# Scan of a hybrid decoder layer: products with the states for both halves first, then one run of 64-column products

## The chip, the cores and the metric

The kernel runs on one core of one Trainium2 chip. The metric is the device time of one execution in microseconds (us). Before the change, three runs took 1005.76, 1002.24 and 1003.0 us; their median is 1003.0 us.

## What is computed

One decoder layer over 512 tokens and 16 learned leading tokens, with 1024 channels: a norm, one wide input projection, two mixing branches side by side (causal pooling, and a Mamba-2 state-space scan), their gated sum, and a squared-ReLU MLP. The change lies in the scan. It has 32 heads of 64 channels in 8 groups of four heads, and works in chunks of 128 tokens:

```python
cb = jnp.einsum("bclgn,bcsgn->bclsg", cf, bf)
y_diag = jnp.einsum("bclsg,bclsgr,bcsgrp->bclgrp", cb, lmat, xdt)
...
y_off = jnp.einsum("bclgn,bcgrpn,bclgr->bclgrp", cf, prev, jnp.exp(a_cs))
y = (y_diag + y_off).reshape(bsz, lp, SSM_HEADS, SSM_HEAD_DIM)[:, pad:]
```

`y_off` is the product of C with the state that a chunk inherits, scaled by a decay. `y_diag` is the product of the decayed and masked scores C·B with x inside the chunk. All is float32.

## The kernel before, in words

Activations lie with channels on the partitions. The input projection takes blocks of 128 output channels: a block of weights is loaded on SP's queue (`block_load`), split into a high part on ScalarE (ACT, L93) and a low part on VectorE (DVE, L95), and multiplied on TensorE (PE) by the high and low parts of the normalized input (`proj`, L191 and L193, result `px` or `pz`). Four buffers each hold high and low parts, so splits can run some blocks ahead of their use. In group 4 the blocks of `out_half` (result `pso`, L127 to L130) and in group 7 those of `out_part` (result `psp`) do the same for the output projection.

The scan goes over the 8 groups. `ssd(g)` is a generator with a step up to each `yield`; `weave` takes a step of the scan and then one of the fill, which is the projection of the next group (`group_proj`), in group 4 also `out_half`, in group 7 `out_part`. The steps of `ssd` that matter here:

- the second step makes the scores (`pc`, L522), the parts of the states (`pst`), the four states `st[0]` to `st[3]`, one after the other on DVE (L538, L539), and multiplies the decays by the masked scores (`dm`, in the buffer of `abc`, L542);
- the third and fourth steps take one half each, that is two heads with 128 channels. For each of the four chunks PE multiplies the state by C (`po`, L550, 128 columns of weights). For each chunk and each of the half's two heads it multiplies x by the decayed scores (`py`, L556, 64 columns of weights; one head goes to partitions 0 to 63 of the result, the other to 64 to 127). DVE joins them: `po` times a decay (L559), plus `py` (L560), plus the skip term (L561), times the gate (L563);
- then come the squares (L567), their sums over channels on PE (`png`, L572, L573), the reciprocal root, and the normalized result as high and low part, which the output projection reads.

`po`, `py`, `pc`, `pst` and the transposes share a pool of four PSUM banks (`psum1`); `px`, `pz`, `pso` and `psp` have a pool of their own (`psum2`, two tiles of two banks). `abc` has one buffer: the load for the next group (L466, on POOL's queue) waits until `py` has been read out of it, and the DMAs of `weight_sums` and `sums_of_u` are put behind that load.

The order on each engine is fixed when the program is built: among the instructions that the builder takes to be ready, the one that stands first in the program goes first. So a `po` whose state is not there yet lets the projection's matmuls go ahead, and comes in between them later. `tc.issue_after(x)` puts an instruction behind x on its engine without a wait of its own. At run time each engine works through its own list in order.

Of the kernel before, what the change touches and what calls it, by code (L numbers as in the profile page):

```python
# [12 lines left out]
ALU = mybir.AluOpType  # L13

P = 128
# [48 lines left out]
def kernel(ctx: ExitStack, tc, xT, x, w, f1, f2, vec, fnw, out):  # L64
    nc = tc.nc
    act, dve, pe, pool = nc.scalar, nc.vector, nc.tensor, nc.gpsimd
# [83 lines left out]
    def col(off, i, n=P):  # L150
        return vs[:n, off + i : off + i + 1]
# [21 lines left out]
    def psum1(name):  # L173
        return psb.tile([P, 512], F32, tag="s", name=name)
# [151 lines left out]
    for i in range(2):  # L326
        pb = psum1(f"pb1_{i}")
        c = slice(3 * i, 3 * i + 3)
        for n in range(2):
            pe.matmul(pb[:, : 3 * NT], ones_r[:NT], dg[n][:, c, :].rearrange("p a b -> p (a b)"),  # L330
                      start=n == 0, stop=n == 1)
# [11 lines left out]
    for c in range(4):  # L343
        r = slice(c * H, (c + 1) * H)
# [113 lines left out]
    def ssd(g, cur):  # L458
# [9 lines left out]
        xdt = gs.tile([P, 4, R, 64], F32, tag="xdt", name=f"xdt{g}")  # L468
# [28 lines left out]
        eb = gs.tile([P, 2, SEQ], F32, tag="eb", name=f"eb{g}")  # L497
# [4 lines left out]
        dm = abc.rearrange("p r (c l) -> p r c l", c=4)  # L502
# [27 lines left out]
        for c in range(3):  # L530
            pe.matmul(pv[c + 1], btok[:, c, :], xdd[:, c, :, :].rearrange("p r d -> p (r d)"),
                      start=True, stop=True)
# [7 lines left out]
        for rs_ in ((slice(0, 2), slice(2, R)) if g == G - 1 else (slice(0, R),)):  # L540
            n = rs_.stop - rs_.start
            masked[g] = dve.tensor_tensor(dm[:, rs_], dm[:, rs_], cbm.unsqueeze(1).to_broadcast([P, n, 4, P]),  # L542
                                          op=ALU.mult)
        yield

        yt = gs.tile([P, 2, SEQ], F32, tag="yt", name=f"yt{g}")
        for i in range(2):
            po = psum1(f"po{g}_{i}")
            for c in range(4):
                pe.matmul(po[:, c * P : (c + 1) * P],  # L550
                          flat(st[c])[:, i * P : (i + 1) * P], ct[:, ctok(c)], start=True, stop=True)
            py = psum1(f"py{g}_{i}")
            for c in range(4):
                for j in range(2):
                    r = 2 * i + j
                    pe.matmul(py[64 * j : 64 * j + 64, c * P : (c + 1) * P],  # L556
                              xdt[:, c, r, :], dm[:, r, c, :], start=True, stop=True)
            y = yt[:, i, :]
            dve.tensor_tensor(y, po, eb[:, i, :], op=ALU.mult)  # L559
            dve.tensor_tensor(y, y, py, op=ALU.add)  # L560
            dve.scalar_tensor_tensor(y, xc[:, i, NM:], col(V_DS, 2 * g + i), y,  # L561
                                     op0=ALU.mult, op1=ALU.add)
            dve.tensor_tensor(y, y, zt[:, i, :], op=ALU.mult)  # L563
            yield
# [14 lines left out]
        for i in range(2):  # L579
            y = yt[:, i, :]  # L580
# [176 lines left out]
    for g in range(G):  # L757
        nxt = group_tiles(g + 1) if g + 1 < G else None
        fill = [group_proj(g + 1, nxt, GATE_AT.get(g))] if nxt else [out_part()]
        if g == 4:  # L760
            fill = [out_half()] + fill
        if g in SUMS_AT:
            fill.append(sums_of_u(SUMS_AT.index(g), g))
        if g in SETS_AT:
            fill.append(weight_sums_at(g))
        weave(ssd(g, cur), fill, 2 if g == 4 else 1)
        cur = nxt
# [700 lines left out]
    c = NC - 1  # L1468
# [10 lines left out]
    end = slice(768, 1024)  # L1479
# [3 lines left out]
    for t in range(4):  # L1483
        T, st = t // 2, slice((t % 2) * P, (t % 2 + 1) * P)
        n = 0
        for half in range(2):
            parts = [(0, 512)] if half == 0 or t < 3 else [(0, 256), (256, 256)]
            for a, m in parts:
# [3 lines left out]
                i = 0  # L1492
# [4 lines left out]
                for k, seg in ((1, (A11, 3)[T]), (0, (A12, A22)[T])):  # L1497
                    wh, wl = wq[k, half]
                    for p in range(2):
                        x0 = p * 512 + a  # L1500
                        f = i == 0 and not (T == 0 and half == 0) and not a
                        i += 1
                        for lhs, rhs in ((hh, wh), (hh, wl), (hl, wh)):
                            pe.matmul(ps, lhs[:, p, seg, st], rhs[:, x0 : x0 + m], start=f and lhs is hh and rhs is wh,
                                      stop=i == 4 and lhs is hl, skip_group_check=True)
# [150 lines left out]
```

## Time and profile before

| | |
|---|---|
| median of three runs | 1003.0 us |
| span of the profiled execution | 1001.4 us |
| its time beside the span | not given by the page |
| granted clock of TensorE, mean | 0.999 |
| DVE busy | 79% of the span |
| ACT busy | 60% of the span |
| POOL busy | 9% of the span |
| DMA moved | 171.47 MB, mean 171 GB/s |

The span is the time from the first to the last instruction of one execution taken by the profiler. A row of the timeline has the start and the duration of an instruction, or of several alike that follow one another (x16), in us. For a tile, a row has the shortest, median and longest duration in ns, and when the first and the last started. A matmul's duration is its latency, and the next one starts before it ends.

### The profile page before, as it was taken

The page shows a single profiled execution, that of the slowest core. Times are in us where ns is not written, and L with a number is a line of the kernel's source. Part 1 is how long each engine was busy: PE and PEld are TensorE (multiplying, and loading weights), DVE is VectorE, ACT ScalarE, POOL GpSimd, SP SyncE. Part 2 cuts the span into 40 slices and gives each one's busy share as a digit, 9 for nine tenths or more (in the row PEclk, how much of TensorE's full clock was granted, in tenths as well). Part 3 has the DMA queues.
Part 4 walks back from the last instruction along what each step waited for, and adds up shares of the span by engine and source line. Part 5 has one row for each costly group of instructions (what it writes and reads, how often), then busy time and mean ns, then how long its engine had stood idle before and what let it go on. Part 6 is the DMA issues. An engine that isn't in the chain of part 4 may idle for free.

```text
span 1001.4 us, 15539 instructions
## 1 busy us (share of the span) xinstructions
PE 993.2 (99%) x6095; PEld 878.3 (88%) x6095; DVE 793.2 (79%) x1147; ACT 602.8 (60%) x840; POOL 88.1 (9%) x148
## 2 busy tenths in 40 slices
PE   9999999999999999999999999999999999999997
PEld 7889898999889998988998888888889999999986
DVE  7988797979736687979789667876988888888885
ACT  8675958595827439483255343368666656656654
POOL 0022101111002011002201001121100000000000
PEclk9999999999999999999999999999999999999999
DMA  7378763678238635417978632879654464454432
GB/s 242 92 281 226 202 185 117 193 188 234 63 104 253 164 99 160 132 38 213 280 203 234 230 105 71 238 194 303 182 189 148 149 189 149 146 187 150 127 105 85
DMA packets 56202, 171.47 MB, mean 171 GB/s; under 512 B 6400, under 2 KB 7744, under 8 KB 55104
## 3 DMA queue, kind: packets, MB, share of 16 engines
q1 hardware_dynamic: 36576, 105.86, 32.5%
q0 software_dynamic: 18832, 63.71, 24.3%
q8 instruction: 48, 0.79, 0.3%
q10 hardware_dynamic: 720, 0.91, 0.3%
q14 instruction: 26, 0.21, 0.1%
HBM read 161.90 MB, written 48.40 MB: 210 GB/s over the span
## 4 chain that ended last, share of the span: by engine, by line
PE 98%; DMA 1%; ACT 0%; DVE 0%; issue 0%; SPq 0%; ACTq 0%
PE px L191 12%; PE px L1291 8%; PE alpha L1359 6%; PE pz L191 6%; PE px L193 6%; PE px L1294 4%; PE alpha L1362 3%; PE pgp L191 3%; PE pz L193 3%; PE pgs L191 3%; PE py L556 2%; PE pso L127 2%; PE po L550 2%; PE wo_alpha L1053 1%; PE pso L128 1%; PE pso L130 1%
## 5 line engine op out<-in xcount | busy, mean ns | idle before, releaser
L93 ACT CAST whi<-raw 128x1024 fp32r<-128x1024 f32 (+2 forms) x98 | 98.5, 1014 | 105.7 <-PE px L193 33.2
L95 DVE TENSOR_TENSOR wlo<-raw,whi 128x1024 fp32r<-128x1024 f32 (+2 forms) x98 | 114.7, 1176 | 50.9 <-ACT whi L93 33.1
L191 PE MATMUL px<-uh,whi 128*128 128x264 f32 (+1 forms) x448 | 113.2, 291 | 0.0
L193 PE MATMUL px<-ul,whi 128*128 128x264 f32 (+1 forms) x448 | 110.5, 285 | 0.0
L191 PEld LDWEIGHTS px<-uh,whi 128*128 128x128 f32 x448 | 84.6, 189 | 1.8 <-issue 1.4
L193 PEld LDWEIGHTS px<-ul,whi 128*128 128x128 f32 x448 | 84.3, 188 | 0.4 <-issue 0.2
L1066 DVE TENSOR_TENSOR ht<-ht,alpha 128x1024 f32<-128x1024 f32 x35 | 42.7, 1219 | 29.1 <-PE alpha L1359 29.1
L989 ACT CAST shi<-rawf 128x1024 fp32r<-128x1024 f32 x42 | 44.2, 1051 | 28.7 <-PE alpha L1362 18.2
L191 PE MATMUL px<-uh,wlo 128*128 128x264 f32 (+1 forms) x448 | 58.5, 283 | 0.0
L191 PEld LDWEIGHTS px<-uh,wlo 128*128 128x128 f32 x448 | 55.9, 188 | 0.0
L1359 PE MATMUL alpha<-shi,hh 128*128 128x512 f32 x140 | 55.2, 394 | 0.0
L1362 PE MATMUL alpha<-shi,hl 128*128 128x512 f32 x140 | 54.7, 391 | 0.0
L990 DVE TENSOR_TENSOR slo<-rawf,shi 128x1024 fp32r<-128x1024 f32 x42 | 51.2, 1218 | 0.6 <-ACT shi L989 0.6
L1294 PE MATMUL px<-vsl,shi 128*128 128x256 f32 x192 | 47.4, 280 | 0.0
L1291 PE MATMUL px<-vsh,shi 128*128 128x256 f32 x192 | 47.4, 281 | 0.0
L193 PE MATMUL pz<-ul,whi 128*128 128x512 f32 x112 | 43.6, 390 | 0.0
L191 PE MATMUL pz<-uh,whi 128*128 128x512 f32 x112 | 43.6, 389 | 0.0
L577 DVE RECIPROCAL rs<-rs 128x128 f32<-128x128 f32 x32 | 27.2, 909 | 13.9 <-ACT rs L575 13.8
L1359 PE MATMUL alpha<-slo,hh 128*128 128x512 f32 x140 | 37.4, 389 | 0.0
L1291 PEld LDWEIGHTS px<-vsh,shi 128*128 128x128 f32 x192 | 36.2, 188 | 0.9
L1294 PEld LDWEIGHTS px<-vsl,shi 128*128 128x128 f32 x192 | 36.1, 188 | 0.9
L1294 PE MATMUL px<-vl,shi 128*128 128x256 f32 x144 | 36.1, 283 | 0.0
(558 smaller groups left out, 2859.1 us busy)
## 6 DMA issues: line engine op xcount, KB each, us to landing
raw<-in_w SPq DMA_DIRECT2D x104, 512.0 KB, 4.4
f_t<-in_f POOLq DMA_DIRECT2D x38, 512.0 KB, 6.7
f_s<-in_f POOLq DMA_DIRECT2D x26, 512.0 KB, 8.6
b<-in_f SPq DMA_DIRECT2D x21, 512.0 KB, 4.6
rawf<-in_f SPq DMA_DIRECT2D x36, 256.0 KB, 3.2
rawf<-f_t SPq DMA_DIRECT2D x36, 256.0 KB, 3.0
abc<-acs_d POOLq DMA_DIRECT2D x8, 1024.0 KB, 7.6
f_t<-f_t POOLq DMA_DIRECT2D x12, 512.0 KB, 4.4
```

What stands on the lines that cost most here:

```text
L93: act.copy(hi[:, c], raw[:, c])
L95: dve.tensor_tensor(lo[:, c], raw[:, c], hi[:, c].bitcast(F32), op=ALU.subtract)
L191: pe.matmul(o, wt, rhs[0][k][:, c], start=part == 0 and k == 0, stop=part == 1 and k == NK - 1)
L193: pe.matmul(o, wt, rhs[1][k][:, c], start=False, stop=False)
L577: dve.reciprocal(rs[:, ctok(c)], rs[:, ctok(c)])
L989: splits.append((act.copy(hi, src), dve.tensor_tensor(lo, src, hi.bitcast(F32), op=ALU.subtract)))
L990: dve.tensor_tensor(lo, src, hi.bitcast(F32), op=ALU.subtract)))
L1066: added[0] = dve.tensor_tensor(o, o, src, op=op)
L1291: pe.matmul(ps, m, f[k][0], start=start and not low and k == 0, stop=stop and low == 1 and k == 3, skip_group_check=True)
L1294: pe.matmul(ps, m, f[k][1], start=False, stop=False, skip_group_check=True)
L1359: pe.matmul(ps[t], hh[:, p, seg, st], m, start=bool(first and not low and p == 0), stop=bool(last and low and p == 1), skip_group_check=True)
L1362: pe.matmul(ps[t], hl[:, p, seg, st], m, start=False, stop=False, skip_group_check=True)
```

## The change

Half 0 and half 1 are no longer taken one after the other on PE. First come the eight `po` products of both halves, then all sixteen `py` products; each `py` is put behind the last `po` of half 1 by `issue_after`. All four result tiles are now held together. The operations of DVE are the same; each half's four still end in a `yield`, so half 1's four still stand behind the next step of the fill in the program.

```diff
         yt = gs.tile([P, 2, SEQ], F32, tag="yt", name=f"yt{g}")
+        po = [psum1(f"po{g}_{i}") for i in range(2)]
         for i in range(2):
-            po = psum1(f"po{g}_{i}")
             for c in range(4):
-                pe.matmul(po[:, c * P : (c + 1) * P],
+                end = pe.matmul(po[i][:, c * P : (c + 1) * P],
                           flat(st[c])[:, i * P : (i + 1) * P], ct[:, ctok(c)], start=True, stop=True)
-            py = psum1(f"py{g}_{i}")
+        py = [psum1(f"py{g}_{i}") for i in range(2)]
+        for i in range(2):
             for c in range(4):
                 for j in range(2):
                     r = 2 * i + j
-                    pe.matmul(py[64 * j : 64 * j + 64, c * P : (c + 1) * P],
-                              xdt[:, c, r, :], dm[:, r, c, :], start=True, stop=True)
+                    with tc.issue_after(end.ins):
+                        pe.matmul(py[i][64 * j : 64 * j + 64, c * P : (c + 1) * P],
+                                  xdt[:, c, r, :], dm[:, r, c, :], start=True, stop=True)
+        for i in range(2):
             y = yt[:, i, :]
-            dve.tensor_tensor(y, po, eb[:, i, :], op=ALU.mult)
-            dve.tensor_tensor(y, y, py, op=ALU.add)
+            dve.tensor_tensor(y, po[i], eb[:, i, :], op=ALU.mult)
+            dve.tensor_tensor(y, y, py[i], op=ALU.add)
             dve.scalar_tensor_tensor(y, xc[:, i, NM:], col(V_DS, 2 * g + i), y,
                                      op0=ALU.mult, op1=ALU.add)
```

## The prediction

> **What bounds the kernel now.** I read first the page's head and its chain of the work that ended last.
>
> ```profile
> span 1001.4 us, 15539 instructions
> PE 993.2 (99%) x6095; PEld 878.3 (88%) x6095; DVE 793.2 (79%) x1147; ACT 602.8 (60%) x840; POOL 88.1 (9%) x148
> ...
> PE 98%; DMA 1%; ACT 0%; DVE 0%; issue 0%; SPq 0%; ACTq 0%
> ```
>
> TensorE (PE) is busy for 993.2 of 1001.4 us, and 98% of the chain runs over it. A busy PE is not PE at its peak, though: matmuls overlap, so time can be lost between their starts while the row still says busy. Next I cut out the scan (from group 0's products to the end of group 7's) and within it 12 us in which group 1 combines its halves.
>
> ```profile
> core 0: us, PE busy (x) PEld busy (x) DVE busy (x) ACT busy (x) POOL busy (x), PEclk, DMA share, GB/s
> 66.00:486.00 420.00, 419.98 (x2822) 376.85 (x2821) 320.30 (x495) 264.39 (x352) 50.09 (x83) 1.00 0.58 171
> 128.00:140.00 12.00, 12.00 (x114) 11.42 (x113) 11.82 (x20) 5.07 (x6) 1.39 (x2) 1.00 0.72 197
> ```
>
> PE is never idle in the scan (419.98 of 420.00 us), at a full clock. So the change gains only where the same matmuls start closer together, and loses only where PE must wait as it does not now. DVE has a quarter of its time free over the scan, but almost none (11.82 of 12.00 us) just where the halves are combined.
>
> **The price of one run of 64-column products.** The tile views name what is moved: an fp32 matmul leaves two records, so the 64 products with the states (po, L550) are 128 records and the 128 products with x (py, L556) are 256.
>
> ```profile
> L550 PE MATMUL po<-ct,st x128: 270/275/377, 85.1 to 451.6; 128*128 128x128 f32 x128
> ...
> L556 PE MATMUL py<-abc,xdt x256: 272/273/324, 85.4 to 452.6; 128*64 128x128 f32 x128
> ```
>
> The durations (273 and 275 ns) are latencies that overlap; what a matmul costs PE is the distance from its start to the next. I take it from the timeline of PE in group 1. First a po among the projection's matmuls, then the second half's po and py and the projection behind them (columns: start, duration, instruction).
>
> ```profile
> 131.04 0.29 PE L191 MATMUL px<-uh,whi 128*128 128x264 f32 x1
> 131.17 0.38 PE L550 MATMUL po<-ct,st 128*128 128x128 f32 x2
> 131.31 0.37 PE L193 MATMUL px<-ul,whi 128*128 128x264 f32 x1
> 131.51 0.29 PE L191 MATMUL px<-uh,whi 128*128 128x264 f32 x1
> 131.64 0.29 PE L193 MATMUL px<-ul,whi 128*128 128x264 f32 x1
> ...
> 136.61 1.06 PE L550 MATMUL po<-ct,st 128*128 128x128 f32 x8
> 137.59 1.09 PE L556 MATMUL py<-abc,xdt 128*64 128x128 f32 x16
> 138.62 0.39 PE L191 MATMUL px<-uh,whi 128*128 128x264 f32 x1
> 138.84 0.29 PE L193 MATMUL px<-ul,whi 128*128 128x264 f32 x1
> 138.97 0.28 PE L191 MATMUL px<-uh,whi 128*128 128x264 f32 x1
> 139.09 0.28 PE L193 MATMUL px<-ul,whi 128*128 128x264 f32 x1
> ```
>
> A px starts 0.12 us after the one before. Eight po take (1.06 - 0.28) / 7 = 0.11 each. So po between px should cost 2 x 0.11 + 0.12 = 0.34 from 131.17 to the second px start; that start is 131.51, which is 0.34 on. Going between px and po costs nothing, though data type, width and PSUM bank all change.
>
> With py it is otherwise. Two 64-column products fill the two halves of the columns together: 16 records stand in 1.09 us, (1.09 - 0.27) / 15 = 0.055 apart, so eight pairs of 0.11 = 0.89. Without a price, po, py and two px would take 8 x 0.11 + 0.89 + 2 x 0.12 = 2.02 us from 136.61, and the third px would start at 138.63. It starts at 138.97. **One run costs about 0.33 us beyond its work**: py starts 0.09 late (137.59 against 136.61 + 0.89), the px behind it 0.10 late, and the next one again 0.10. The same sum on the other unbroken runs gives 0.32 to 0.34.
>
> The Trainium skill, "TensorEngine Tiling (Array Packing)", section Key Properties, says that a change of tiling mode, not merely of tile, drains TensorE. The 0.33 us at the two changes agrees; by that rule two runs laid end to end pay once, which no row here shows.
>
> **How many runs go.** Eight groups have two halves, and one run is broken in two, so there are 17. Here are the first and last, and the two groups that differ from the rest.
>
> ```profile
> 85.38 1.09 PE L556 MATMUL py<-abc,xdt 128*64 128x128 f32 x16
> ...
> 286.41 1.09 PE L556 MATMUL py<-abc,xdt 128*64 128x128 f32 x16
> 293.01 1.06 PE L550 MATMUL po<-ct,st 128*128 128x128 f32 x8
> 299.50 1.09 PE L556 MATMUL py<-abc,xdt 128*64 128x128 f32 x16
> ...
> 406.25 0.37 PE L191 MATMUL px<-uh,whi 128*128 128x264 f32 x1
> 406.55 0.65 PE L556 MATMUL py<-abc,xdt 128*64 128x128 f32 x6
> 407.13 0.49 PE L550 MATMUL po<-ct,st 128*128 128x128 f32 x2
> 407.55 0.87 PE L556 MATMUL py<-abc,xdt 128*64 128x128 f32 x10
> 408.35 0.39 PE L193 MATMUL px<-ul,whi 128*128 128x264 f32 x1
> ...
> 451.80 1.09 PE L556 MATMUL py<-abc,xdt 128*64 128x128 f32 x16
> ```
>
> In group 6 a po stands inside the first half's py. From 406.55 to 408.35 PE spends 1.80 us on eight py pairs and one po, whose work is 0.89 + 0.22 = 1.11: 0.69 lost. Add 0.18 ahead (406.25 to 406.55, less a px's 0.12) and the 0.10 that the second px behind loses: 0.97, which is 0.31 above two runs' price of 0.66.
>
> After the change every py stands behind the last po, and nothing of the group can come between. The full gain is 17 - 8 = 9 runs. In group 4 I expect less. Each run there stands alone between two blocks of the output projection (pso), 6.5 us apart: the order fixed at build time puts the scan's steps only into the gaps that it expects between blocks. A gap that took 16 records now may not take 32, so I count two runs still for group 4. **Sum: 8 runs x 0.33 = 2.6 us**, plus the 0.3 of group 6: 2.9 us.
>
> **What lies beside it.** The four po of half 1 move ahead; their price was nil in the rows above and stays nil (between 0 and 0.34 us a group, a run's price; the po row is nearest). The join of the two runs costs between 0 and 0.33; I take 0, as within one run the pairs follow at 0.11 even though the column half changes. The hold on PSUM grows: po and py of both halves take all four banks of their pool at once. The next to ask is the group's sum of squares, which needs both halves anyway, so no wait is added.
>
> The wait added: py of half 0 stands behind po's last chunk, which needs the last state from DVE (L539). That po stood in PE's queue before too, and PE did not wait for it (419.98 of 420.00), so 0, at most one gap between chunks, 2.2 us (131.17 to 133.35 in group 1), for each group that the order misjudges. Behind it would stand py and the projection. The abc load of the next group (L466, POOL's queue) waits for the last py, which now comes some us earlier; with it come the DMAs queued behind it. They land among the weight loads; the splits' lead, below, covers that.
>
> **Covers for DVE.** Before, half 0's py was long done when DVE came to add it; now it ends later. In group 1 half 0's last po is at 133.35:
>
> ```profile
> 133.35 0.39 PE L550 MATMUL po<-ct,st 128*128 128x128 f32 x2
> ...
> 133.78 0.69 DVE L559 TENSOR_TENSOR yt<-po,eb 128x512 f32<-128x512 f32 x1
> 134.39 1.22 DVE L95 TENSOR_TENSOR wlo<-raw,whi 128x1024 fp32r<-128x1024 f32 x1
> 135.52 0.68 DVE L560 TENSOR_TENSOR yt<-yt,py 128x512 f32<-128x512 f32 x1
> ...
> 405.78 1.21 DVE L95 TENSOR_TENSOR wlo<-raw,whi 128x1024 fp32r<-128x1024 f32 x1
> ...
> 412.44 2.09 PE L191 MATMUL px<-uh,wlo 128*128 128x264 f32 x16
> ```
>
> With the last po of both halves (2 x 0.22) and py of half 0 (0.09 + 0.89, and 0.16 for the last one's latency), py is there at about 134.9, before DVE adds it at 135.52. Where no split stands between, DVE waits up to 1.9 us (both halves' py, 0.09 + 1.78). Behind L560 in DVE's queue are the splits of weights that PE uses later. In group 6, the tightest I found, a split ends at 406.99 and its low half is first used at 412.44: a lead of 5.4 us, more than 1.9. So I cost DVE's wait at nothing.
>
> **Rivals.**
> 1. *Forecast, 0.66*: 7 to 9 runs go, 2.3 to 3.3 us. 1001.4 - 2.9 = 998.5 for the profiled execution. The page gives its span and no time around it; the runs' median, 1003.0, lies 1.6 above, which I keep: 1003.0 - 2.9 = 1000.1, and with half a us of scatter 999.2 to 1001.2 alone.
> 2. *The change doesn't do what it says, 0.16*: the order fixed at build time still breaks py up between blocks, as in groups 4 and 6 now. For: both groups. Against: once the last po is out nothing of the group is missing. 0 to 4 runs go: 1003.0 - 0.7 = 1002.3.
> 3. *Slower, 0.05*: DVE waits at L560 in every group, and the splits behind it come too late. Price 8 x 1.9 = 15.2 us, less 2.9: 1015.3. It decides from a delay of 5.4 us in a group. For it: DVE's 11.82 of 12.00. Against: the lead.
> 4. *Evacuation binds, 0.03*: PE waits for a bank while DVE reads half 0 (L559 and L560, 0.69 + 0.68 = 1.37 us), 8 x 1.37 - 2.9 = 8.1 more: 1011.1. Against: the projections have banks of their own. The Trainium skill, "TensorEngine Tiling (Array Packing)", section PSUM Bottleneck, warns of this: tiling speeds up TensorE but not the emptying of PSUM.
> 5. *Faster by more than 0.5%, 0.10*: all 17 runs together cost 17 x 0.33 + 0.3 = 5.9 us, so 997.1 is the floor unless other stalls go. It also takes in scatter: three runs lie 1002.24 to 1005.76.
>
> **How the numbers follow.** The likeliest is 1000.1. The range 998.0 to 1003.2 holds rivals 1 and 2 whole. Half a per cent (5.0 us) is about what a measurement of this kernel tells from no change: faster 0.10 (5), same 0.82 (1, 2), slower 0.08 (3, 4).
>
> **What would show it.** Right: in the after-trace one row of 32 py records in most groups, behind po, and the distance from po to the third px some 0.33 us above its work, once; PE's busy time in the scan shorter by the same 2 to 3 us. Wrong: PE idle before px with DVE's wlo as releaser (3), or before L572 (4); py still in 16 or more runs (2); a price that comes back at the join.

## The result and the profile after

The changed kernel takes 1009.94 us (median of five runs, 1008.54 to 1010.46) against 1003.0 before: **ratio 1.0061, 95% interval 1.0051 to 1.0072**. It is slower by 6 to 7 us; the prediction was 1000.1 us, with 1003.2 as the upper end. The profiled execution took 1010.25 us by itself, 1.75 more than its span. A line number of `ssd` from L552 on is two or three higher after the change: `py` is L558, DVE's four operations are L562, L563, L564 and L566, the cast `th` is L754.

From the page of the changed kernel, its head and the shares of the chain that ended last:

```profile
span 1008.5 us, 15519 instructions
...
PE 993.0 (98%) x6095; PEld 878.8 (87%) x6095; DVE 792.6 (79%) x1147; ACT 602.8 (60%) x840; POOL 88.1 (9%) x148
...
PE 97%; ACT 2%; DMA 0%; DVE 0%; issue 0%; ACTq 0%
```

PE's busy time is the same (993.0 against 993.2), and the span is 7.1 us longer, so what came is idle time. (The time saved at the runs is in that sum too, set off by a stretch of slower matmuls, below: without the stall, in the next section but one, PE is busy for 991.2 us.) ACT has 2% of a chain in which it had none. The view of waits, for PE (us in total, times, longest), says where; these are the four longest:

```profile
PE pso L127 <- ACT acc L641: 2.9, 1, 2.9
PE pso L127 <- ACT yh L587: 2.4, 1, 2.4
PE pdt L233 <- DVE ones_r L138: 1.5, 1, 1.5
PE psp L127 <- DVE acc L670: 1.4, 1, 1.4
```

The wait for `ones_r` is that of before. New are two waits in group 4's output projection (`pso`) and one in group 7's (`psp`). Elsewhere in the scan PE waits 0.3 us or less at a time. To follow the loss I take a landmark that each group has once, the transposes `ptb` (L474). Their row in the tile view, first and last start at its end, is this before the change:

```profile
L474 PE MATMUL ptb<-ident,bt x24: 270/272/273, 69.0 to 433.9; 128*128 128x128 f32 x24
```

and this after it:

```profile
L474 PE MATMUL ptb<-ident,bt x24: 270/272/273, 68.8 to 439.9; 128*128 128x128 f32 x24
```

In group 7 the changed kernel is 6.0 us late. In group 4, by the timeline of PE, it was still early; before, then after:

```profile
258.91 0.49 PE L474 MATMUL ptb<-ident,bt 128*128 128x128 f32 x3
```

```profile
257.42 0.49 PE L474 MATMUL ptb<-ident,bt 128*128 128x128 f32 x3
```

So the changed kernel was 1.49 us ahead by 257 us (0.2 us of it from before the scan: group 0's landmark stands at 68.8 instead of 69.0), and the loss lies behind it. The windows around it (after the window come its length and PE's busy time with its matmuls; the third number from the end is the granted clock), before, then after with group 7 as well:

```profile
252.00:300.00 48.00, 48.00 (x248) 39.43 (x248) 26.39 (x38) 26.80 (x38) 0.00 (x0) 1.00 0.27 78
```

```profile
252.00:300.00 48.00, 42.22 (x215) 33.83 (x214) 30.02 (x46) 29.47 (x41) 4.80 (x9) 0.96 0.34 107
...
440.00:470.00 30.00, 28.64 (x164) 23.45 (x162) 28.79 (x42) 16.66 (x20) 3.19 (x6) 1.00 0.40 117
```

In group 4 PE does 33 matmuls fewer in the same 48 us: 5.8 us idle and a lower granted clock (0.96). In group 7 it is idle for 1.4 us.

**The price of a run was right.** Group 1 after the change, by the timeline of PE:

```profile
134.79 0.61 PE L550 MATMUL po<-ct,st 128*128 128x128 f32 x4
135.32 1.97 PE L558 MATMUL py<-abc,xdt 128*64 128x128 f32 x32
137.22 0.87 PE L191 MATMUL px<-uh,wlo 128*128 128x264 f32 x5
137.93 0.28 PE L191 MATMUL px<-uh,whi 128*128 128x264 f32 x1
```

The work from 134.79 to 137.93 is 4 x 0.11 + 32 x 0.055 + 5 x 0.12 = 2.80 us; it takes 3.14. Those 0.34 us are paid once for 32 records where they had been paid for 16, and the join costs nothing. All eight groups have one such row of 32, group 4 too.

### The profile page after: what moved, and what is told of

It is laid out like the page before. It is cut to its first block, busy times and chain, and to the rows that moved or that the text cites. A ratio compares the mean times of both kernels' runs of the same rounds, so it can differ in the third digit from the quotient of the medians.

```text
span 1008.5 us, 15519 instructions
## 1 busy us (share of the span) xinstructions
PE 993.0 (98%) x6095; PEld 878.8 (87%) x6095; DVE 792.6 (79%) x1147; ACT 602.8 (60%) x840; POOL 88.1 (9%) x148
## 4 chain that ended last, share of the span: by engine, by line
PE 97%; ACT 2%; DMA 0%; DVE 0%; issue 0%; ACTq 0%
PE px L191 12%; PE px L1294 8%; PE alpha L1362 6%; PE pz L191 6%; PE px L193 6%; PE px L1297 4%; PE alpha L1365 3%; PE pgp L191 3%; PE pz L193 3%; PE pgs L191 3%; PE py L558 2%; PE wo_alpha L1056 1%; PE pf L128 1%; PE pf L127 1%; PE pgp L193 1%; PE pgs L193 1%
```

## Where the time is lost: one chain through every queue

Here are the queues that lead to group 4, first before the change. POOL's timeline (start, duration, instruction, in brackets the idle time ahead and what ended it):

```profile
200.14 0.54 POOL L713 DMA_DIRECT2D f_t<-in_f  x1
...
228.51 0.82 POOL L721 DMA_DIRECT2D f_t<-in_f  x1 [3.64 <-DMA f_t<-f_t]
236.54 0.59 POOL L466 DMA_DIRECT2D abc<-acs_d  x1 [7.21 <-PE py L556]
```

POOL does the sums of group 3 (`weight_sums`, eight DMAs that wait for one another), is through at 229.3, and waits 7.2 us for `py` before it issues group 4's load of `abc`. After the change:

```profile
211.10 0.54 POOL L716 DMA_DIRECT2D f_t<-in_f  x1
...
241.12 0.81 POOL L724 DMA_DIRECT2D f_t<-in_f  x1 [4.45 <-DMA f_t<-f_t]
241.67 0.84 POOL L466 DMA_DIRECT2D abc<-acs_d  x1
```

No idle time and no `py` stands ahead of the load. PE's timeline has `py` of group 3 done 10 us before:

```profile
229.24 1.97 PE L558 MATMUL py<-abc,xdt 128*64 128x128 f32 x32
```

The load now waits for POOL's own list, which started its sums 11 us late. What waits for the load is ACT:

```profile
241.50 0.61 ACT L303 CAST qhg<-sqg 128x512 fp32r<-128x512 f32 x1
250.60 1.28 ACT L501 ACT_TABLE_LOAD   x1 [8.49 <-DMA abc<-acs_d]
...
264.12 1.12 ACT L587 CAST yh<-yt 128x512 fp32r<-128x512 f32 x2
```

ACT stands still for 8.5 us with `eb` at the head of its list, and `rs`, `yh` and the copies of `pso` behind it. PE reaches them too early:

```profile
264.77 0.51 PE L127 MATMUL pso<-yh,whi 128*128 128x512 f32 x1 [2.40 <-ACT yh L587]
...
273.46 0.50 PE L127 MATMUL pso<-yh,whi 128*128 128x512 f32 x1 [2.87 <-ACT acc L641]
273.80 0.39 PE L128 MATMUL pso<-yl,whi 128*128 128x512 f32 x1
...
274.60 0.63 PE L127 MATMUL pso<-yh,whi 128*128 128x512 f32 x1
275.02 0.63 PE L128 MATMUL pso<-yl,whi 128*128 128x512 f32 x1
...
277.58 0.48 PE L128 MATMUL pso<-yl,whi 128*128 128x512 f32 x1
```

And why do the sums start late? They stand on POOL behind the stores of group 2's `th`, which ACT casts, from `ua` and `ub`, which DVE makes. DVE's timeline in group 2, before:

```profile
185.02 0.42 DVE L742 TENSOR_TENSOR ua<-ub,ua 128x260 f32<-128x260 f32 x1
...
187.78 0.68 DVE L559 TENSOR_TENSOR yt<-po,eb 128x512 f32<-128x512 f32 x1
```

and after:

```profile
185.38 0.74 DVE L564 SCALAR_TENSOR_TENSOR yt<-xc,vs,yt 128x512 f32<-128x512 f32 x1
...
195.49 0.42 DVE L745 TENSOR_TENSOR ua<-ub,ua 128x260 f32<-128x260 f32 x1
```

Before, `ua` was made ahead of half 1's operations. Now both halves become ready together, half 1's go first, and `ua` falls 10.5 us back. On ACT the cast falls back further, behind the next group's `eb`, a gate of the fill (`m`) and this group's `rs`; before, then after:

```profile
186.25 0.61 ACT L751 CAST th<-ua 128x520 fp32r<-128x520 f32 x1
```

```profile
201.29 0.69 ACT L578 ACTIVATE rs<-png,eps 128x512 f32<-128x512 f32 x1
201.88 0.61 ACT L754 CAST th<-ua 128x520 fp32r<-128x520 f32 x1
```

**My theory**: the new order on PE makes the builder put DVE's and ACT's lists in another order; POOL's list, which keeps its own order, runs 11 to 12 us late for it, has 7 us of slack, and hands the rest on through the load to ACT and PE in group 4. **Rivals**: the new order of PE and ACT stalls by itself and the late load is a companion; or the joined run costs something in PE.

## Experiments: is it the late load?

**The load off POOL's queue.** The changed kernel, with group 4's load alone issued from SP's queue. Its control does the same to the kernel before.

```diff
-        abc_load[g] = nc.gpsimd.dma_start(abc, ...)
+        abc_load[g] = (nc.sync if g == 4 else nc.gpsimd).dma_start(abc, ...)
```

> The changed kernel, with only group 4's abc load issued from SP's queue instead of POOL's; the order on PE, ACT and DVE is the same. Queue theory: the load starts soon after py of group 3 ends (231 us), the waits at eb and at pso go: 1000 to 1002. Rival (own order of the changed kernel): 1008 to 1011.

> Control: the kernel before with group 4's abc load on SP's queue. There the load was held by py (it left at 236.5, just behind py's end), not by the queue, so nothing changes: 1002.9 to 1003.9. If the move were a gain by itself, it would show here as 1.5 us or more.

Measured: 1001.64 us, ratio to the kernel before 0.9981 (0.9972 to 0.9990); the control 0.9994 (0.9985 to 1.0002), no difference. In the first, SP's timeline has the load, and these are all of PE's waits:

```profile
231.22 0.33 SPq L466 DMA_DIRECT2D abc<-acs_d  x1
```

```profile
PE pdt L233 <- DVE ones_r L138: 1.5, 1, 1.5
PE psp L127 <- DVE acc L670: 1.4, 1, 1.4
```

The load goes out 10.5 us earlier and both waits at `pso` are gone, with the lists of PE, ACT and DVE in the same order as in the changed kernel. The sums on POOL still start at 211.07. So it is the load, and neither the order of PE nor the sums.

**The sums out of its way.** The changed kernel with group 3's set of sums done after the scan; its control is the kernel before with the same edit.

```diff
-SETS_AT = {0: 2, 1: 1, 3: 1, 5: 1, 6: 1}
-SETS_POOL = 3
+SETS_AT = {0: 2, 1: 1, 5: 1, 6: 1}
+SETS_POOL = 4
```

> The changed kernel, with group 3's set of weight sums (8 DMAs on POOL's queue ahead of group 4's abc load) moved to the pooling stage. Queue theory (group 4's abc load is late because POOL's queue stands behind group 3's casts and weight sums, and ACT stands at eb until it lands): the load is issued near 231 us instead of 241.7, ACT's 8.5 us wait at eb goes, the pso waits in group 4 (2.9, 2.4) go, and the time falls by about 8 us, to 1000 to 1002. Rival (the changed kernel's own order on ACT and DVE makes group 3's result late, wherever the load stands): yh of group 3 stays near 264 us, PE still waits about 5 us in group 4, time 1008 to 1011.

> Control: the kernel before with the same set of weight sums moved. Queue theory: its abc load of group 4 waited for py (issued right behind py's end at 236.5), not for POOL's queue, so no change: 1002 to 1004. If moving the set were a gain by itself (less DMA traffic in the scan), it would show here as 2 us or more.

Measured: 1001.65 us, ratio 0.9984 (0.9976 to 0.9993); control 0.9999 (0.9990 to 1.0008). The load goes out at 231.98, held by `py` again, and no wait at `pso` is left. Two ways to free the load give the same time, and neither gives the kernel before anything.

**A late load in the old order.** The kernel before with two sets of sums in group 3 instead of one (`3: 2`, and one less at the end).

> The kernel before, PE's order untouched, with a second set of the weight sums put into group 3, so that on POOL's queue the load of abc for group 4 stands behind two sets. If a late load of abc for group 4 is by itself enough to stop PE (my theory), the old order stalls too: the load starts 12 to 20 us later than 236.5 us, PE waits at pso of group 4 for ACT's yh and acc, and the time is 1012 to 1030. If the stall needs the new order on PE, and the late load is only its companion, the time stays at 1003 to 1005.

Measured: 1030.35 us, ratio 1.0275 (1.0261 to 1.0289). From the timelines of POOL, ACT and PE:

```profile
258.25 0.58 POOL L466 DMA_DIRECT2D abc<-acs_d  x1
```

```profile
270.19 0.62 ACT L751 CAST th<-ub 128x520 fp32r<-128x520 f32 x1 [27.13 <-DMA t_d13h<-th]
```

```profile
271.38 0.80 PE L572 MATMUL png<-qhg,ones_r 128*128 128x512 f32 x1 [24.21 <-ACT qhg L303]
```

The load comes 21.7 us late and the time grows by 27.5 us, with PE's old order. The place was not the one expected, and the time is just above the range: here ACT is held by the store of `th`, which stands behind the sums and the load on POOL, and PE stops at `png` instead of `pso`. ACT stops ahead of `eb`, so it is not the load itself that it waits for. What is shown is that POOL's list, run late, stops ACT and through it PE, whatever the order of PE.

## Experiments: why is the load late?

**The cast ahead of eb.** The changed kernel, with the next group's `eb` put behind this group's first `th` on ACT.

```diff
+            with tc.issue_after(cast[g - 1].ins) if g - 1 in cast else nullcontext():
                 act.activation(eb[js, :, :], ap[js, :, j, :], AF.Exp)
```

> The changed kernel, with each group's eb (L501) put behind the cast th of the group before on ACT, as it stood in the kernel before. Queue theory, taken one step back (the casts slid behind eb on ACT, so POOL's queue, which stores their results, stood still for 19 us instead of 8 and issued group 3's weight sums 11 us late): POOL's t_d13h waits fall from 97 us in all to 65 or less, group 3's weight sums start near 200 us, the load is no longer late: 1000 to 1003. If the casts' place isn't the reason: 1008 to 1011.

POOL's timeline:

```profile
201.27 0.54 POOL L718 DMA_DIRECT2D f_t<-in_f  x1
...
233.50 0.84 POOL L466 DMA_DIRECT2D abc<-acs_d  x1
```

With the cast at 193.08 the sums start at 201.27 (200.14 before the change, 211.10 after) and the load goes out at 233.50, 8 us earlier than in the changed kernel though still 3.6 us behind the end of `py` (229.90); POOL's waits for `th` (`t_d13h`) fall from 97.3 to 65.7 us. So the link from the place of the casts to the load is shown. DVE's `ua` came earlier as well (189.59 instead of 195.49), so DVE's share and ACT's are not told apart. PE's waits at `pso` are gone, but a new one of 2.9 us stands at `pz`, for DVE's `xc`. The median is 1006.04 us, between the two forecasts; the runs spread from 1002.35 to 1010.49 us, ratio 1.0025 (1.0009 to 1.0041), and the profiled one (1004.67) is of the shorter ones. On the link the run decides; on the time it does not.

**The sums ahead of the stores.** The changed kernel, with group 3's sums put on POOL directly behind that group's own load.

```diff
-        with tc.issue_after(sums_load.get(g, abc_load[g]).ins):
+        with tc.issue_after((abc_load[g] if g == 3 else sums_load.get(g, abc_load[g])).ins):
```

> The changed kernel, with the sums of group 3 put directly behind that group's own load of abc, so that on POOL they no longer stand behind the stores of group 2's transposed weights and the loads held by ACT's casts. Theory (the sums start late because they stand behind those): they start near 200 us as before the change, the load of abc for group 4 starts when the last py of group 3 is read (231 to 234 us), pso does not wait, 1001.0 to 1002.5. Rival (the sums themselves became slower, or the stall comes from ACT's order alone): 1007 to 1010.

A miss: 1013.06 us, ratio 1.0104 (1.0090 to 1.0117). POOL, ACT and PE:

```profile
184.05 0.53 POOL L716 DMA_DIRECT2D f_t<-in_f  x1
...
214.32 0.58 POOL L756 DMA_DIRECT2D t_d13h<-th  x1 [0.17 <-issue]
```

```profile
220.59 0.62 ACT L754 CAST th<-ub 128x520 fp32r<-128x520 f32 x1 [12.97 <-DMA t_d13h<-th]
```

```profile
225.25 1.19 PE L529 MATMUL pst<-xddm,btm 16*128 16x256 f32 x2 [7.80 <-DVE xddm L494]
```

The sums end in time, but now the store of `th` stands behind them; its buffer is not free for the second cast, ACT stops for 13 us, and PE for 7.8, in group 3. The load is held by `py` again, and no wait at `pso` is left. I had asked only who waits for the load, and not who waits for what I moved past: the same fault as in the prediction.

**Some groups only.** The changed order in groups 1 to 3 alone, and in all but these (`g in MERGED` chooses the order).

> The change in groups 1 to 3 alone, all loads where they were. Queue theory (the casts of these groups slide behind eb on ACT, POOL's queue stands, group 4's abc load is late): three runs go (-1.0), and the late load brings PE waits of 2 to 8 us at the start of group 4, so 1004 to 1010. Rival (the loss comes from joining groups 4 to 7): 1002.4, no wait in group 4.

> The change in groups 0, 4, 5, 6 and 7 alone. Queue theory: the casts of groups 1 to 3 stay ahead of the eb of the next group on ACT, the load is not late; four to five runs go (-1.5, with group 6's broken run), group 7's wait costs 1.0: 1002.5 to 1003.3. Rival: 1008 to 1010, as the loss would come from these groups.

Measured: 1014.01 us, ratio 1.0102 (1.0087 to 1.0116), more than expected, and 1008.58, ratio 1.0051 (1.0035 to 1.0068). The second missed: I had the chain begin in groups 1 to 3, whose order is that of before here. Yet POOL's timeline of the second has

```profile
210.31 0.54 POOL L729 DMA_DIRECT2D f_t<-in_f  x1
...
242.84 0.84 POOL L467 DMA_DIRECT2D abc<-acs_d  x1
```

so both variants start the sums 10 to 11 us late. The part of my theory that placed the cause in certain groups fell. The second's time is the one that the rival named. But PE waits only 1.5 us at `pso` there, beside 1.2 at `po` and 1.4 at `psp`, and with all groups joined and the load freed, above, only the wait at `psp` is left; so the joining of these groups does not by itself cost 5 us. How its loss divides is not shown. The order at build time reacts to a change anywhere upstream, and two quite different mixtures delay the casts of group 2. Which of its choices tips over, and why just there, these runs leave open.

## Experiments: group 7, and the best version

In group 7 the fill's next block waits for DVE to empty a bank (`acc`), and DVE is busy with the states. PE's timeline before, and after the load was moved to SP:

```profile
447.30 1.09 PE L556 MATMUL py<-abc,xdt 128*64 128x128 f32 x16
...
449.51 0.50 PE L127 MATMUL psp<-yh,whi 128*128 128x512 f32 x1
```

```profile
446.73 0.50 PE L127 MATMUL psp<-yh,whi 128*128 128x512 f32 x1 [1.35 <-DVE acc L670]
```

Half 0's `py` used to fill that time; now it stands behind the last `po`. Three kernels bear on what this is worth: group 7 alone changed; all but group 7 changed, with the load on SP; and all but group 7, with the sums moved away.

> The kernel before with the changed order in group 7 alone; POOL's order up to there is that of before. Theory (group 7's old half 0 filled PE while psp waited for a bank): PE waits about 1.4 us at psp, one run's 0.33 us is saved, the time is 0.7 to 1.3 us above before, ratio 1.0007 to 1.0013. Rival (the wait was hidden anyway, only the run counts): ratio 0.9997.

> The changed kernel with group 4's abc load on SP's queue (as in the run before) and group 7 alone in the old order. Theory on group 7 (in the old order half 0's py filled the time in which PE waits for DVE to free a psp tile; with all py behind the last po that filler is gone and PE waits 1.35 us, more than the 0.33 that the joined run saves): the psp wait of 1.4 us goes, and the time falls by about 1.0 us below the 1001.6 of the run before, to 1000.4 to 1000.9; the ratio to the kernel before is 0.997. Rival (the wait comes from something else in the order): psp still waits, 1001.3 to 1002.

> The changed order in groups 0 to 6, the old one in group 7, and group 3's set of sums moved to the end on POOL. Theory: neither the stall of group 4 nor the wait for psp of group 7; all the joined runs' gain is left: 1000.5 to 1001.3, ratio 0.997 to 0.998. Rival (group 7's order is worth nothing): 1001.6 as with the set moved alone.

Group 7 alone: 1004.16 us, ratio 1.0008 (0.9999 to 1.0018), where theory expected 1.0007 to 1.0013; PE waits 1.1 us, but at `po` for DVE's state:

```profile
449.30 0.71 PE L553 MATMUL po<-ct,st 128*128 128x128 f32 x4 [1.13 <-DVE st L540]
```

All but group 7 with the load on SP: **1000.98 us, ratio 0.9971 (0.9959 to 0.9982), the lowest time measured**; PE is never idle from 252 to 300 and from 440 to 470 us, so the wait at `psp` does come from the new order in group 7. With the sums away: 1001.65, 0.9986 (0.9977 to 0.9995), no better than with group 7 joined (1001.65), though the wait at `psp` is gone there too; why is not shown. The idle time in group 7 is shown in the traces; what it costs at the end is about 1 us or nothing, and the intervals overlap.

## Why the prediction was wrong

- **Price and number of runs: right.** 0.33 us forecast, 0.34 measured, join free. Group 4 was to keep two runs and has one, so nine runs went, not eight.
- **The gain: there, but smaller than its sum.** With the load freed the landmark in group 7 stands at 431.4 against 433.9, 2.5 us earlier, of which 0.4 were there ahead of the scan (68.67 against 69.03 at group 0's landmark). So groups 0 to 6 gained 2.1 us, where their eight runs and group 6's 0.3 make 2.9. Groups 0 to 3 gave 1.1 to 1.3, about the four runs' 1.3; group 6 gave 0.4 (43.63 against 44.01 us to the next landmark) of its 0.97, partly because `pz` starts 0.30 us later behind the last `px`. The lowest time measured is 2.45 us below the kernel before beside it (1000.98 against 1003.43; by the interval, 1.8 to 4.1).
- **The step that failed** is in "What lies beside it": "The abc load of the next group (L466, POOL's queue) waits for the last py, which now comes some us earlier; with it come the DMAs queued behind it." I took `py` for the only thing that the load waits for, and never asked what else stands ahead of it. POOL's own list was through 7.2 us before `py`; after the change it was through 12 us later (241.7 against 229.3), so the load went out 5.1 us later (241.67 against 236.54) where I had it come earlier, and reached ACT (`eb`) and PE (`pso`) too late. PE lost 8.5 us by it: with the load freed and all else the same, the landmark in group 4 stands at the same time (257.41 against 257.42), and the one in group 7 at 431.4 instead of 439.9. Of the 8.5, 5.8 are idle time, and the slower starts, below, make up 1.6; the remaining 1.1 us is not taken apart.
- **"Covers for DVE": right in its figure, too narrow in what it covered.** No wait at a split arose (rival 3), but behind `yt` in DVE's list I looked only for splits. The operation that moved was `ua`, 10.5 us. That half 1's four operations stand behind the next step of the fill holds for the program's text; in DVE's list of group 2 they now go ahead of `ua`.
- **Rivals 3 and 4** put the slower side, with a chance of 0.08 together, at DVE and at PSUM. The waits that would have shown them are absent; no wait before `png` came. The rival that was needed, a reordering of the other engines' lists, had no place in the list.
- **Order of group 7**: a wait like the one costed at "0, at most one gap between chunks" did come there, 1.4 us, but at `psp`, for DVE's `acc`: the fill beside the scan was itself waiting. With group 7 alone changed it stood at `po`, for the state, as the prediction had it, and took 1.1 us.

## What to carry to other kernels

Where a builder orders each engine's list by readiness, a change of one engine's order changes the lists of all: before costing it at nothing, follow each in-order queue from the moved step to the next place where it meets the critical engine, and write down its slack there (here 7.2 us on POOL, against 12 us of delay). The bracket behind a row names what came last, not all that it waits for; the time at which the queue's own list was through is the second number to read. A transfer that others wait for does not belong behind a chain of transfers that nobody in the scan waits for: one word, moving one load to another queue, turned +0.6% into -0.2%.

## What the runs showed of the hardware

After the wait of 2.87 us in group 4 the granted clock of TensorE is 0.50 for 3.41 us. The window, with the columns as above:

```profile
274.35:277.76 3.41, 3.41 (x10) 2.66 (x9) 3.41 (x5) 2.17 (x4) 0.00 (x0) 0.50 0.02 1
```

The matmuls of `pso` there take 0.63 us instead of 0.39 and start 0.42 or 0.43 apart instead of 0.23, from 274.60 to 277.58; with the step ahead of these and the one behind, that adds 1.6 us to the wait. After 2.40 us of idle time nine us earlier no such stretch is seen, nor after the 2.89 us at `pz` in the run with the cast ahead of `eb` (clock 1.00 from 250.11 on). With the sums ahead of the stores, 7.80 us of idle time came with 10.24 us at 0.50 (221.91 to 232.15). So an idle PE can cost more than its idle time, and at 2 to 3 us the length of the wait does not tell whether it will. The Trainium skill, "TensorE: Matmul & The Clock Gate", Part 1, section What's actually happening, says that after an idle window of about 3.4 us the clock falls to half and rises again after about as long a busy one; the 3.41 us at 0.50 agree with the second, the 2.87 us of idle time ahead of them are less than the figure of the first, and here the measurement decides.

A set of sums of 0.5 to 0.8 us per DMA on POOL takes 29 to 31 us of its queue (200.14 to 229.3 before, 211.10 to 241.9 after), since most of them wait for an earlier one to land. POOL is busy 9% of the span, and its queue is the one that decided.
